# Hybrid decoder layer on one core: transposes of the SSD features pinned behind later matmul groups, early low parts on VectorE, first q and k projection traced ahead of the SSD output projection

## Chip, cores and metric

One core of a Trainium2 chip runs the whole kernel in one launch. The metric is the device time of that core in microseconds (us), lower is better.

## What is computed

One layer, 512 tokens, width 1024, float32 in and out. In short:

```python
proj = rms_norm(x) @ w_in                      # z | x,B,C | dt | q | k | v | f
y_ssd = ssd_mixer(xbc, z, dt)                  # conv(4) + silu, chunked scan, gate, group norm
y_fox = fox_mixer(q, k, v, f)                  # 16 heads, causal softmax with forget gates
x = x + concat(y_ssd, y_fox) @ w_out
x = x + conv_gated_mlp(rms_norm(x), w_up, w_down)
```

The SSD mixer has two groups of 8 heads. Its features (x, B, C: 1536 columns) go through a causal convolution over four tokens and a silu; then four chunks of 128 tokens are scanned one after the other, and the result is gated by silu(z) and normalised.

## The kernel before

**Matmuls in three passes.** Each float32 operand is split into a high part `h` (rounded to fp32r) and a low part `l` (the rest). `mm3` (line 108) issues h·h, h·l and l·h. `load_split` (line 99) brings one 128x1024 block of weights (512 KB) on SP's queue into `wraw` (5 buffers), ScalarE casts it to `wh` (line 104), and VectorE or GpSimd subtracts to give `wl` (line 105); `wh` and `wl` have 3 buffers each. Which engine subtracts is read, call by call, from the letters in the table `LOW_PART` (line 35): d is VectorE (DVE), p is GpSimd (POOL), and a key that is not in the table gives p. So the key feat (feature tiles) uses POOL for its first call only, z0 (the z projection of group 0, four blocks) has no entry and uses POOL four times, z1 is pdpd, o0 is d, and qk0 has no entry: four times POOL.

**The order of the work.** The program is traced in the order of the Python code, but it is not issued in that order: the framework's scheduler simulates the engines and picks, on each engine, the ready instruction of highest priority (earlier traced is higher; what is inside `urgent()` is raised by 2000). What it fixes is the order of each engine's queue. On the chip an engine takes its queue strictly in that order, and an instruction at the head that is not ready holds up the rest.

**The stages around the change.**

- Four feature tiles are made early (line 604, 605): j = 8 (B of group 0), 10 (C of group 0), 0 and 1 (x).
- `ssd_proj(g)` (line 338) goes over six feature tiles of group g: B, C, then four x tiles. Each is 24 matmuls of 512 columns, then on VectorE a multiply (L347), three taps of the convolution (L354) and the last step of the silu (L359), with two activations on ScalarE between (L350, L358). B and x are then transposed to token order: four PE transposes into one PSUM bank `xT` (lines 361 to 363; the pool `po` has a single bank), copied out by ScalarE (L368 for x, L370 for B). After the six tiles come two calls of `token_block` (line 321) for z, each 96 matmuls of 256 columns on two weight blocks, whose results are gated into `gz` (L377 to L379).
- `ssd_scan(g)` (line 388, urgent) runs the four chunks. Chunk c loads its row of decays (`sc`, L398), masks it on POOL (L407), takes exponentials (L412), multiplies (L415), then PE `yd` (L418), `yo` (L424), `st` (L431), VectorE steps on `y` and `xdt` (L421, L429, L439), and at the end the PE transposes `yT` (L449), which ScalarE and VectorE write into the operand pair `msh`, `msl` (L451, L452). That pair has one buffer: scan 1 writes it only when `out_proj((0, 1), m0)` has read the result of scan 0.
- `dt_f` (line 265) is a VectorE chain that ends in the decays `cs`, on which every chunk waits.
- The lines 604 to 623 fix the tracing order: early tiles, dt_f, ssd_proj(0), scan 0, ssd_proj(1), out_proj((0, 1), m0), scan 1, then `project(0)` (q and k of the first head group, two token_blocks, evacuated by L463, L465, L466, L471 and a power on POOL, L123) and `project_v(0)`. After that the attention heads follow (from L498 on), with the remaining projections as filler work, then the MLP.

Of the kernel before, what the change touches and what calls it, by code (L numbers as in the profile page):

```python
# [8 lines left out]
F32 = mybir.dt.float32  # L9
# [6 lines left out]
P = 128  # L16
# [3 lines left out]
NTB = SEQ // P  # L20
# [12 lines left out]
AHEAD = 2000  # L33
WARM = 8
LOW_PART = {
    "feat": "pddddddddp",
    "o0": "d",
    "o2": "d",
    "o4": "pd",
# [16 lines left out]
def tile_hybrid_layer(  # L56
# [20 lines left out]
    act, dve, pool, pe = nc.scalar, nc.vector, nc.gpsimd, nc.tensor  # L77
# [5 lines left out]
    po = ctx.enter_context(tc.tile_pool(name="po", bufs=1, space=PSUM))  # L83
# [42 lines left out]
    ident = cp.tile([P, P], F32, tag="ident", name="ident")  # L126
# [77 lines left out]
    for k in range(NK):  # L204
        pe.matmul(pdt[:64, :], wdt[:, k, :], xh[:, k, :], start=k == 0, stop=False, skip_group_check=True)
        pe.matmul(pdt[:32, :], wdt[:, k, 0:32], xl[:, k, :], start=False, stop=k == NK - 1, skip_group_check=True)
        c = slice(k * P, (k + 1) * P)
# [8 lines left out]
    def feature_tile(src, o=None):  # L216
        h, l = src if isinstance(src, tuple) else load_split(src, sub=low_part("feat"))
        o = bank() if o is None else o
        for k in range(NK):
            mm3(  # L220
                o, h[:, k * P : (k + 1) * P], l[:, k * P : (k + 1) * P], xh[:, k, :], xl[:, k, :],
                k == 0, k == NK - 1,
            )
        return o
# [13 lines left out]
    def out_proj(pairs, m, halves=(0, 1)):  # L238
        for half in halves:
            ws = [load_split(wout[pair, half], sub=low_part("o%d" % pairs[0])) for pair in pairs]  # L240
            banks = {}
            for t0 in (0, 2):
                for n, (h, l) in enumerate(ws):
                    for tb in (t0, t0 + 1):
                        s = slice(tb * P, (tb + 1) * P)
                        if n == 0:
                            banks[tb] = bank("po")
                        for j in range(2):
                            k = 2 * n + j
                            c = slice(j * 512, (j + 1) * 512)  # L250
                            mm3(
                                banks[tb], m[k][0][:, s], m[k][1][:, s], h[:, c], l[:, c],
                                k == 0, k == 2 * len(pairs) - 1,
                            )
                        if n == len(ws) - 1:
                            dst = x2[:, tb, half * 512 : (half + 1) * 512]
                            dve.tensor_add(dst, banks[tb], dst)
# [4 lines left out]
    def tmp(tag, name):  # L262
        return pss.tile([P, 512], F32, tag=tag, name=name, bufs=4 if tag == "t" else 2)
# [54 lines left out]
        act.activation(eacs, tokS[:, 1, :, 0:16], AF.Exp)  # L318
        nc.sync.dma_start(dsk, ssd_d[0:1, :].to_broadcast([P, SSD_HEADS]))

    def token_block(src, key="tb"):
        tiles = [bank("pq") for _ in range(2)]
        for kh in range(2):
            h, l = load_split(src[kh], sub=low_part(key))
            for b in range(2):
                for j in range(4):
                    k = 4 * kh + j
                    for c in range(2):
                        tb = 2 * b + c
                        s = slice(tb * P, (tb + 1) * P)  # L330
                        mm3(
                            tiles[b][:, c * 256 : (c + 1) * 256], xh[:, k, s], xl[:, k, s],
                            h[:, j * 256 : (j + 1) * 256], l[:, j * 256 : (j + 1) * 256],
                            k == 0 and c == 0, k == NK - 1, grouped=False,
                        )
        return tiles

    def ssd_proj(g):
        x_tok = [pss.tile([P, 512], F32, tag="x_tok", name="x_tok", bufs=7) for _ in range(NTB)]
        bT = pss.tile([P, SEQ], F32, tag="bT", name="bT", bufs=2)  # L340
        cT = pss.tile([P, SEQ], F32, tag="cT", name="cT", bufs=2)
        b_tok = pss.tile([P, NTB, P], F32, tag="b_tok", name="b_tok", bufs=2)
        gz = [pss.tile([P, 512], F32, tag="gz", name="gz", bufs=6) for _ in range(NTB)]
        for j in [8 + g, 10 + g] + list(range(4 * g, 4 * g + 4)):
            o = early.pop(j, None) or feature_tile(wxbc[j])
            xp = tmp("t", "xp")
            dve.tensor_mul(xp, o, R)  # L347
            dst = bT if j in (8, 9) else cT if j > 9 else tmp("t", "xs")
            cw = C_SCW + 4 * j
            act.activation(  # L350
                dst, xp, AF.Identity, scale=half_w[:, cw + 3 : cw + 4], bias=half_w[:, C_SCB + j : C_SCB + j + 1]
            )
            for s in range(1, 4):
                dve.scalar_tensor_tensor(  # L354
                    out=dst[:, s:], in0=xp[:, : SEQ - s], scalar=half_w[:, cw + 3 - s : cw + 4 - s], in1=dst[:, s:],
                    op0=ALU.mult, op1=ALU.add,
                )
            act.activation(xp, dst, AF.Tanh)  # L358
            dve.scalar_tensor_tensor(out=dst, in0=xp, scalar=1.0, in1=dst, op0=ALU.add, op1=ALU.mult)  # L359
            if j < 10:  # L360
                t = po.tile([P, 512], F32, tag="o", name="xT")
                for c in range(NTB):
                    pe.transpose(t[:, c * P : (c + 1) * P], dst[:, c * P : (c + 1) * P], ident)
                tv = t.rearrange("p (c f) -> p c f", c=NTB)
                if j < 8:
                    jj = j - 4 * g
                    for c in range(NTB):
                        act.copy(x_tok[c][:, jj * P : (jj + 1) * P], tv[:, c, :])  # L368
                else:
                    act.copy(b_tok, tv)  # L370
        for half in range(2):
            tiles = token_block(wz[2 * g + half], "z%d" % g)
            for tb in range(NTB):
                o = tiles[tb // 2][:, (tb % 2) * 256 : (tb % 2 + 1) * 256]
                dst = gz[tb][:, half * 256 : (half + 1) * 256]
                th = pss.tile([P, 256], F32, tag="th", name="th", bufs=2)
                act.activation(dst, o, AF.Copy, scale=rhalf[:, tb : tb + 1])  # L377
                act.activation(th, o, AF.Tanh, scale=rhalf[:, tb : tb + 1])
                dve.scalar_tensor_tensor(out=dst, in0=th, scalar=1.0, in1=dst, op0=ALU.add, op1=ALU.mult)  # L379
        return x_tok, bT, cT, b_tok, gz  # L380
# [220 lines left out]
    def urgent():  # L601
        return tc.high_priority(AHEAD)
# [5 lines left out]
    with urgent():  # L608
        m0 = ssd_scan(0, *st0)
    st1 = ssd_proj(1)  # L610
    out_proj((0, 1), m0)
    with urgent():
        m1 = ssd_scan(1, *st1)
    qk, vs = {}, {}

    def project(g):
        qk[g] = [qk_proj(g, 0), qk_proj(g, 1)]

    def project_v(g):
        vs[g] = v_proj(g)  # L620

    project(0)
    project_v(0)
    pss_ctx.close()
    pf_ctx = ExitStack()
# [51 lines left out]
    for half in range(2):  # L677
        c = slice(half * 512, (half + 1) * 512)
        ks = slice(half * 4, half * 4 + 4)
        for tb in range(NTB):  # L680
            s = slice(tb * P, (tb + 1) * P)
            with urgent():
                xw = pa.tile([P, 512], F32, tag="tok", name="xw", bufs=4)
                (dve if (half, tb) == (1, 3) else pool).tensor_tensor(out=xw, in0=x2[:, tb, c], in1=nw[:, c], op=ALU.mult)
                t = mbank("hT")
# [113 lines left out]
    for j in range(NH):  # L799
        g, val = gated(j)  # L800
# [180 lines left out]
```

## Time and profile before

| what | value |
|---|---|
| median of 3 runs | 815.75 us (815.62 to 817.22) |
| the profiled execution: its own time | 818.96 us |
| the profiled execution: span, first to last instruction | 817.2 us |
| granted TensorE clock | 0.999 |
| busy PE, DVE, ACT, POOL (us) | 803.1, 610.4, 437.2, 265.9 |

PE is the engine of the matmuls, PEld its weight loads, DVE is VectorE, ACT ScalarE, POOL GpSimd, SP the engine on whose queue the loads are issued. L12 is line 12 of the kernel. Names such as `xT<-ident,xs` give the tile that is written and those read. In a timeline each row has the start, the duration, the engine, line, operation, tiles, shapes and how many like instructions are merged; in brackets stands the idle time of the engine just before and what released it. Ends of matmuls are modelled: two matmuls that follow each other without a gap overlap in the rows, so the distance of two starts is the surer measure.

### The profile page before, as it was taken

To read this page: it belongs to the slowest core of one execution; us is meant where nothing else is said; L and a number is where in the kernel's file an instruction comes from. 1 tells how busy PE (TensorE), PEld (TensorE's weight loads), DVE (VectorE), ACT (ScalarE), POOL (GpSimd) and SP (SyncE) were. 2 spreads that over 40 slices of the span, in tenths; PEclk is the share of its full clock that TensorE was granted. 3 is DMA by queue.
4 is the path that set the end of the run, shared out by engine and by line. 5 is a ranking of instruction groups with operands and counts; after the bars stand their busy time and mean duration, and the time that the engine had idled before them with its cause. 6 is when DMAs were issued, how large, how long until landed. Compare 5 with 4: busy or idle time off the path is not lost.

```text
span 817.2 us, 12396 instructions
## 1 busy us (share of the span) xinstructions
PE 803.1 (98%) x4591; PEld 697.9 (85%) x4591; DVE 610.4 (75%) x987; ACT 437.2 (54%) x835; POOL 265.9 (33%) x268
## 2 busy tenths in 40 slices
PE   8989999999999999999999999999999999999997
PEld 6878878889999999898898888888888888888886
DVE  4696898656689898898996858666776666787844
ACT  7447656434387777585574364443444334556532
POOL 0233343255256635143211414333223333043120
PEclk9999999999999999999999999999999999999999
DMA  8524323323233433333321272233222322399983
GB/s 324 193 79 134 103 78 105 116 78 129 90 98 98 133 108 99 114 96 124 104 78 53 85 196 93 91 103 103 98 85 102 103 92 89 90 256 184 218 188 94
DMA packets 31404, 98.22 MB, mean 120 GB/s; under 512 B 4016, under 2 KB 5104, under 8 KB 31344
## 3 DMA queue, kind: packets, MB, share of 16 engines
q1 hardware_dynamic: 27456, 85.38, 32.1%
q0 software_dynamic: 3456, 11.54, 8.0%
q8 instruction: 36, 0.59, 0.3%
q10 hardware_dynamic: 432, 0.52, 0.2%
q14 instruction: 24, 0.20, 0.1%
HBM read 91.56 MB, written 2.20 MB: 115 GB/s over the span
## 4 chain that ended last, share of the span: by engine, by line
PE 85%; DVE 10%; DMA 2%; ACT 1%; issue 1%; POOL 0%; SPq 0%; DVEq 0%; ACTq 0%
PE up L111 29%; PE pq L111 19%; PE po L111 10%; PE Y L111 6%; PE X L111 4%; PE Z L111 4%; DVE xs L354 3%; PE o L587 2%; PE pT L573 2%; PE g L111 2%; PE S L547 1%; PE S L546 1%; DVE wl L105 1%; PE yd L418 1%; DVE xp L347 1%; DVE cT L354 1%
## 5 line engine op out<-in xcount | busy, mean ns | idle before, releaser
L104 ACT CAST wh<-wraw 128x1024 fp32r<-128x1024 f32 x103 | 108.5, 1053 | 141.2 <-PE up L111 78.6
L111 PE MATMUL pq<-wh,xl 128*128 128x256 f32 x512 | 148.3, 290 | 0.0
L111 PE MATMUL pq<-wh,xh 128*128 128x256 f32 x512 | 146.1, 286 | 0.0
L111 PE MATMUL pq<-wl,xh 128*128 128x256 f32 x512 | 145.7, 285 | 0.0
L111 PE MATMUL up<-hl,wh 128*128 128x512 f32 (+1 forms) x368 | 140.0, 381 | 0.0
L111 PE MATMUL up<-hh,wh 128*128 128x512 f32 (+1 forms) x368 | 139.9, 381 | 0.0
L111 PE MATMUL up<-hh,wl 128*128 128x512 f32 (+1 forms) x368 | 139.7, 380 | 0.0
L105 DVE TENSOR_TENSOR wl<-wraw,wh 128x1024 fp32r<-128x1024 f32 x81 | 104.0, 1284 | 32.3 <-ACT wh L104 27.9
L111 PEld LDWEIGHTS pq<-wh,xh 128*128 128x128 f32 x512 | 97.5, 190 | 2.1 <-issue 1.7
L111 PEld LDWEIGHTS pq<-wh,xl 128*128 128x128 f32 x512 | 97.5, 190 | 2.1 <-issue 1.4
L111 PEld LDWEIGHTS pq<-wl,xh 128*128 128x128 f32 x512 | 97.5, 190 | 0.6 <-issue 0.2
L111 PEld LDWEIGHTS up<-hl,wh 128*128 128x128 f32 x368 | 69.2, 188 | 13.4 <-issue 0.2
L111 PEld LDWEIGHTS up<-hh,wh 128*128 128x128 f32 x368 | 69.1, 188 | 13.3 <-issue 0.2
L111 PEld LDWEIGHTS up<-hh,wl 128*128 128x128 f32 x368 | 69.2, 188 | 13.1
L105 POOL TENSOR_TENSOR wl<-wraw,wh 128x1024 fp32r<-128x1024 f32 x22 | 54.0, 2459 | 71.8 <-ACT wh L104 57.2
L775 DVE TENSOR_TENSOR up<-up,R 128x512 f32<-128x512 f32 x44 | 30.3, 691 | 59.5 <-PE up L111 59.5
L780 DVE SCALAR_TENSOR_TENSOR ua<-up,pc,ua 128x511 f32<-128x511 f32 (+1 forms) x88 | 66.3, 758 | 1.4
L552 ACT ACTIVATE prob<-prob,nm 128x128 f32<-128x128 f32 (+1 forms) x64 | 35.9, 564 | 24.9 <-DVE nm L548 24.8
L736 ACT CAST wh<-T 128x1024 fp32r<-128x1024 f32 (+1 forms) x30 | 29.3, 977 | 36.8 <-PE Z L111 15.3
L737 DVE TENSOR_TENSOR wl<-T,wh 128x1024 fp32r<-128x1024 f32 (+1 forms) x30 | 33.7, 1133 | 19.1 <-ACT wh L736 18.8
L533 POOL TENSOR_SCALAR bias<-cum,tokS 128x256 f32<-128x256 f32 (+1 forms) x32 | 22.9, 725 | 71.6 <-DVE nm L548 71.6
L790 POOL TENSOR_TENSOR ua<-ua 128x512 f32<-128x512 f32 x11 | 15.0, 1363 | 92.6 <-DVE ua L780 92.6
(236 smaller groups left out, 1848.0 us busy)
## 6 DMA issues: line engine op xcount, KB each, us to landing
wraw<-in_wup_dram SPq DMA_DIRECT2D x44, 512.0 KB, 3.3
wraw<-in_wqkv_dram SPq DMA_DIRECT2D x24, 512.0 KB, 3.3
T<-in_wdown_dram POOLq DMA_DIRECT2D x20, 512.0 KB, 7.0
wraw<-in_wout_dram SPq DMA_DIRECT2D x16, 512.0 KB, 3.3
wraw<-in_wxbc_dram SPq DMA_DIRECT2D x11, 512.0 KB, 5.6
T<-in_wdown_dram SPq DMA_DIRECT2D x10, 512.0 KB, 5.5
wraw<-in_wdown_dram SPq DMA_DIRECT2D x10, 512.0 KB, 3.6
wraw<-in_wz_dram SPq DMA_DIRECT2D x8, 512.0 KB, 3.8
```

What stands on the lines that cost most here:

```text
L104: act.copy(h, r)
L105: (sub or dve).tensor_tensor(out=l, in0=r, in1=raw(h), op=ALU.subtract)
L111: ins = pe.matmul(o, a, b, start=start and n == 0, stop=stop and n == 2, **kw)
L354: dve.scalar_tensor_tensor(out=dst[:, s:], in0=xp[:, : SEQ - s], scalar=half_w[:, cw + 3 - s : cw + 4 - s], in1=dst[:, s:], op0=ALU.mult, ...
L533: (dve if qb == 2 else pool).tensor_scalar(out=b, in0=cum[:, :n], scalar1=-1.0, scalar2=edge, op0=ALU.mult, op1=ALU.add)
L552: act.activation(p, p, AF.Exp, scale=-1.0, bias=nm[:, qb : qb + 1], accum_out=sm[:, qb : qb + 1])
L573: pe.transpose(t[:, w : w + P], prob[:, o : o + P], ident)
L587: pe.matmul(cols[:m], v[:, kb, lh, vc], pt[:, s], start=kb == 0 and n == 0, stop=kb == NTB - 1, skip_group_check=True,)
L736: act.copy(h[:, :n], src[:, :n])
L737: dve.tensor_tensor(out=l[:, :n], in0=src[:, :n], in1=raw(h[:, :n]), op=ALU.subtract)
L775: dve.tensor_mul(xp, o, R2)
L780: dve.scalar_tensor_tensor(out=a[:, s:], in0=xp[:, : SEQ - s], scalar=pc[:, cw + 2 - s : cw + 3 - s], in1=a[:, s:], op0=ALU.mult, op1=ALU.add,
```

## The change

It has three parts. First, `LOW_PART` has only d for feat and for z0. Second, the transposes of B and x are no longer traced right after each tile: a queue `late` holds them, and each set of four is traced behind a later group of matmuls and pinned there. The pin (`keep_in_program_order`) is an edge of the order in PE's queue to the instruction that was traced just before; it fixes the earliest place in the queue, not the latest. B goes behind the group of the third x tile, the first x tile behind the group of the fourth, the other three x tiles behind pieces of the z projection (a piece is 24 matmuls, numbered 0 to 7 over both halves): pieces 1, 3 and 6 for group 0, pieces 1, 3 and 5 for group 1. Third, `project(0)` is traced ahead of `out_proj((0, 1), m0)` and of scan 1.

```diff
@@ LOW_PART
-    "feat": "pddddddddp",
+    "feat": "d",
+    "z0": "d",
@@ def token_block
-    def token_block(src, key="tb"):
+    def token_block(src, key="tb", behind=None):
...
                             k == 0 and c == 0, k == NK - 1, grouped=False,
                         )
+                if behind is not None:
+                    behind(2 * kh + b)
         return tiles
@@ def ssd_proj
-        for j in [8 + g, 10 + g] + list(range(4 * g, 4 * g + 4)):
+        def to_tokens(j, src):
+            t = po.tile([P, 512], F32, tag="o", name="xT")
+            for c in range(NTB):
+                tc.keep_in_program_order(
+                    pe.transpose(t[:, c * P : (c + 1) * P], src[:, c * P : (c + 1) * P], ident)
+                )
+            tv = t.rearrange("p (c f) -> p c f", c=NTB)
+            if j < 8:
+                jj = j - 4 * g
+                for c in range(NTB):
+                    act.copy(x_tok[c][:, jj * P : (jj + 1) * P], tv[:, c, :])
+            else:
+                act.copy(b_tok, tv)
+
+        late = []
+        for n, j in enumerate([8 + g, 10 + g] + list(range(4 * g, 4 * g + 4))):
             o = early.pop(j, None) or feature_tile(wxbc[j])
+            if n > 3:
+                to_tokens(*late.pop(0))
             xp = tmp("t", "xp")
...
             if j < 10:
-                t = po.tile([P, 512], F32, tag="o", name="xT")
-                for c in range(NTB):
-                    pe.transpose(t[:, c * P : (c + 1) * P], dst[:, c * P : (c + 1) * P], ident)
...
+                late.append((j, dst))
         for half in range(2):
-            tiles = token_block(wz[2 * g + half], "z%d" % g)
+            tiles = token_block(
+                wz[2 * g + half], "z%d" % g,
+                lambda piece: to_tokens(*late.pop(0)) if 4 * half + piece in (1, 3, 5 if g else 6) else None,
+            )
@@ the order of tracing
     st1 = ssd_proj(1)
+    qk, vs = {}, {}
...
+    project(0)
     out_proj((0, 1), m0)
     with urgent():
         m1 = ssd_scan(1, *st1)
-    qk, vs = {}, {}
...
-    project(0)
     project_v(0)
```

## Rows read from the trace of the kernel before

**Rows 1.** The page's busy time of each engine: busy us, share of the span, instructions.
```profile
PE 803.1 (98%) x4591; PEld 697.9 (85%) x4591; DVE 610.4 (75%) x987; ACT 437.2 (54%) x835; POOL 265.9 (33%) x268
```

**Rows 2.** Busy time of each engine in stretches of the span: start and end in us, length, then busy us (and instructions) of PE, PEld, DVE, ACT, POOL, the granted clock, the DMA share and GB/s.
```profile
40.00:60.00 20.00, 17.06 (x113) 15.29 (x112) 19.68 (x34) 8.69 (x16) 6.36 (x4) 1.00 0.25 80
...
80.00:140.00 60.00, 57.55 (x331) 48.32 (x331) 54.27 (x72) 35.47 (x88) 20.77 (x15) 1.00 0.29 99
140.00:230.00 90.00, 90.00 (x635) 82.19 (x635) 54.83 (x87) 39.53 (x90) 36.83 (x27) 1.00 0.29 97
230.00:340.00 110.00, 110.00 (x852) 105.73 (x851) 98.70 (x225) 83.53 (x192) 56.35 (x76) 1.00 0.38 111
340.00:465.00 125.00, 124.53 (x786) 110.09 (x785) 105.87 (x218) 71.86 (x153) 33.64 (x41) 1.00 0.30 93
```

**Rows 3.** PE's timeline between 47 and 70 us: the z projection of group 0 (`pq`) and the transposes `xT`.
```profile
47.83 0.27 PE L111 MATMUL pq<-wh,xh 128*128 128x256 f32 x1
...
49.97 0.28 PE L111 MATMUL pq<-wh,xh 128*128 128x256 f32 x1
50.09 0.28 PE L111 MATMUL pq<-wl,xh 128*128 128x256 f32 x1
51.88 0.66 PE L363 MATMUL xT<-ident,xs 128*128 128x128 f32 x4 [1.52 <-ACT b_tok L370]
...
57.56 0.66 PE L363 MATMUL xT<-ident,xs 128*128 128x128 f32 x4 [1.42 <-ACT x_tok L368]
...
64.07 0.63 PE L363 MATMUL xT<-ident,xs 128*128 128x128 f32 x4 [1.41 <-DVE xs L359]
...
69.26 0.60 PE L363 MATMUL xT<-ident,xs 128*128 128x128 f32 x4
```

**Rows 4.** PE's timeline further on: the waits of over half a microsecond between 80 and 235 us.
```profile
119.33 0.63 PE L363 MATMUL xT<-ident,xs 128*128 128x128 f32 x4 [1.26 <-ACT wh L104]
...
125.79 2.00 PE L418 MATMUL yd<-xdt,sc 128*128 128x64 f32 x16 [0.59 <-DVE sc L415]
...
132.65 1.10 PE L431 MATMUL st<-xdt,b_tok 128*128 128x512 f32 x2 [0.53 <-DVE xdt L429]
```

**Rows 5.** DVE's timeline: the long rows between 36 and 62 us, and before or behind them rows of the same kind of instruction; the first is a low part on DVE, the second the instruction that follows it.
```profile
31.21 1.23 DVE L105 TENSOR_TENSOR wl<-wraw,wh 128x1024 fp32r<-128x1024 f32 x1 [4.20 <-PE rbc L144]
32.35 1.28 DVE L347 TENSOR_TENSOR xp<-g,R 128x512 f32<-128x512 f32 x2
...
36.53 0.73 DVE L354 SCALAR_TENSOR_TENSOR xs<-xp,half_w,xs 128x511 f32<-128x511 f32 x1
...
37.60 2.96 DVE L354 SCALAR_TENSOR_TENSOR cT<-xp,half_w,cT 128x510 f32<-128x510 f32 x1
...
45.22 0.69 DVE L359 SCALAR_TENSOR_TENSOR cT<-xp,cT 128x512 f32<-128x512 f32 x1
...
46.43 2.29 DVE L359 SCALAR_TENSOR_TENSOR xs<-xp,xs 128x512 f32<-128x512 f32 x1
...
53.37 2.04 DVE L294 TENSOR_TENSOR e<-e,den 128x128 f32<-128x128 f32 x1
...
55.94 0.28 DVE L296 TENSOR_TENSOR q<-e 128x128 f32<-128x128 f32 x1
...
58.92 2.89 DVE L354 SCALAR_TENSOR_TENSOR xs<-xp,half_w,xs 128x509 f32<-128x509 f32 x1
```

**Rows 6.** POOL's timeline between 20 and 62 us: the low part of the second x tile, then the four of z0.
```profile
22.82 2.54 POOL L105 TENSOR_TENSOR wl<-wraw,wh 128x1024 fp32r<-128x1024 f32 x1 [0.44 <-ACT wh L104]
37.63 2.39 POOL L105 TENSOR_TENSOR wl<-wraw,wh 128x1024 fp32r<-128x1024 f32 x1 [12.27 <-DVE u L286]
45.70 2.47 POOL L105 TENSOR_TENSOR wl<-wraw,wh 128x1024 fp32r<-128x1024 f32 x1 [5.68 <-ACT wh L104]
52.86 2.41 POOL L105 TENSOR_TENSOR wl<-wraw,wh 128x1024 fp32r<-128x1024 f32 x1 [4.69 <-ACT wh L104]
58.54 2.73 POOL L105 TENSOR_TENSOR wl<-wraw,wh 128x1024 fp32r<-128x1024 f32 x1 [3.27 <-ACT wh L104]
```

**Rows 7.** DVE's timeline: the multiply of the decays of chunk 2 of scan 0, on which the `yd` of rows 4 waits.
```profile
124.52 1.21 DVE L415 TENSOR_TENSOR sc<-sc,cb 128x1024 f32<-128x1024 f32 x1
```

**Rows 8.** PE at the SSD output projection (`po`): its first matmul, the last chunk's transposes of scan 0, the first chunk's of scan 1, the first matmul of q and k, and the last chunk's transposes of scan 1.
```profile
153.97 0.40 PE L111 MATMUL po<-wh,msh 128*128 128x512 f32 x1
...
155.60 0.60 PE L449 MATMUL yT<-ident,y 128*128 128x128 f32 x4
...
178.97 0.60 PE L449 MATMUL yT<-ident,y 128*128 128x128 f32 x4
...
180.32 0.28 PE L111 MATMUL pq<-wh,xh 128*128 128x256 f32 x1
...
228.88 0.60 PE L449 MATMUL yT<-ident,y 128*128 128x128 f32 x4
```

**Rows 9.** ScalarE's timeline: the first write of scan 1's result.
```profile
180.34 0.59 ACT L451 CAST msh<-yT 128x512 fp32r<-128x512 f32 x1 [0.80 <-PE po L111]
```

**Rows 10.** POOL's timeline: the mask of a chunk of scan 1 at the head of the queue, the low part of q and k behind it, and the power for the norm of q.
```profile
169.00 1.09 POOL L407 TENSOR_SCALAR_AFFINE_SELECT sc<-sc 128x1024 f32<-128x1024 f32 x1 [11.66 <-DVE dte L405]
170.06 2.38 POOL L105 TENSOR_TENSOR wl<-wraw,wh 128x1024 fp32r<-128x1024 f32 x1
...
197.82 2.92 POOL L123 TENSOR_TENSOR ms<-ms,mhalf 128x16 f32<-128x16 f32 x1 [2.51 <-DVE ms L122]
```

More of the change, by code (lines that the diff above doesn't have):

```diff
@@ L360, in ssd_proj @@
             if j < 10:
-                t = po.tile([P, 512], F32, tag="o", name="xT")
-                for c in range(NTB):
-                    pe.transpose(t[:, c * P : (c + 1) * P], dst[:, c * P : (c + 1) * P], ident)
[L364 to L370, printed above, removed]
+                late.append((j, dst))
         for half in range(2):
-            tiles = token_block(wz[2 * g + half], "z%d" % g)
+            tiles = token_block(
+                wz[2 * g + half], "z%d" % g,
+                lambda piece: to_tokens(*late.pop(0)) if 4 * half + piece in (1, 3, 5 if g else 6) else None,
+            )
             for tb in range(NTB):
@@ L610, in tile_hybrid_layer @@
     st1 = ssd_proj(1)
-    out_proj((0, 1), m0)
-    with urgent():
-        m1 = ssd_scan(1, *st1)
     qk, vs = {}, {}
@@ L622, in tile_hybrid_layer @@
     project(0)
+    out_proj((0, 1), m0)
+    with urgent():
+        m1 = ssd_scan(1, *st1)
     project_v(0)
```

## The prediction

> **What bounds the kernel now.** I read the page's busy time first: PE has 803.1 of 817.2 us [rows 1], so what is not PE work is 14 us in all, and a change that leaves the matmuls as they are can win only from PE's waits. Then the stretches [rows 2]: between 140 and 340 us PE is busy all the time, and it loses 0.5 us between 340 and 465; the losses lie ahead of 140, where PE has 17.06 of 20 us (40 to 60) and 57.55 of 60 us (80 to 140) while DVE is the fullest engine beside it (19.68 of 20 and 54.27 of 60). So I went through PE's timeline there. Three of the four sets of x transposes of group 0 come after 1.52, 1.42 and 1.41 us of idle PE [rows 3], 4.35 us together; later one set of group 1, a `yd` and an `st` of scan 0 wait 1.26, 0.59 and 0.53 us [rows 4], 2.38 us. That is 6.73 us. The idle numbers are a little short, since ends of matmuls are modelled: the first wait is 50.09 to 51.88 from start to start, 1.79 us where 49.97 to 50.09 shows 0.12 as usual, so 1.67 and not 1.52. With 0.15 more for each of six waits, 7.6 us is all that there is to win.
>
> Next, why the transposes are late. The releasers are ScalarE's copies out of the single `xT` bank and DVE's last step of the silu, so DVE's chain is behind, and DVE's timeline shows where it lost time [rows 5]: a tap of the convolution takes 2.96 us where its neighbour takes 0.73, a silu step 2.29 instead of 0.69, a small multiply 2.04 (its like: 0.28), another tap 2.89. Each of the four begins within 0.8 us of one of POOL's low parts of z0, which run 37.63, 45.70, 52.86 and 58.54 us, for 2.39 to 2.73 us [rows 6]. So while POOL subtracts, DVE stands still: 2.23 + 1.60 + 1.76 + 2.15 = 7.7 us lost. PE's queue order was fixed by a simulation; that PE waits at these transposes says that DVE runs later on the chip than there.
>
> **Part 1, five low parts from POOL to DVE.** Removed: the 7.7 us of DVE standing still. Added: four low parts on DVE at 1.14 us (31.21 to 32.35, start to start [rows 5]), 4.6 us. DVE's chain of the x tiles and of `cs` ends 7.7 − 4.6 = 3.1 us earlier, though it takes work on. The fifth (the second x tile, 22.82 us on POOL [rows 6]) meets a DVE that stands idle 4.20 us before 31.21 [rows 5]: nothing. The `wl` of z0 is there 1.2 us sooner; PE did not wait for it. And the planner, which did not see the standing still, now sees 4.6 us more of DVE work, so it puts what hangs on DVE later into PE's queue, while on the chip DVE is 3.1 us earlier: the two come 7.7 us nearer. That is more than the 4.35 us of waits in this stretch, so I take these waits as gone: 4.35 + 3 × 0.15 = 4.8 us. Bounds: 0 and 4.8.
>
> What the page of the Trainium skill "SBUF — State Buffer", section Who interferes with whom, says of this: a DVE instruction with two SBUF inputs and a GpSimd instruction that reads SBUF exclude each other, and whichever comes second blocks until the first has finished. By it each low part would cost DVE POOL's whole instruction, 10.0 us for the four, and DVE would come out 5.4 us earlier instead of 3.1; the rows show less, and in the first pair it is DVE's row that starts first (37.60 against 37.63), yet DVE that is long. I go by the rows.
>
> **Part 2, the pins.** No instruction is added; the order of 40 transposes moves. Counting z0's matmuls from 47.83 at 0.12 us each, without the waits and the transposes, the four x sets of group 0 stand behind about 20, 50, 88 and 122 of them [rows 3]. The new earliest places are 0, 48, 96 and 168. So the pins move nothing for the first two sets (they rest on part 1), move the third by 8 × 0.12 = 1 us, and the fourth, which did not wait, by 46 × 0.12 = 5.5 us. That later `x_tok` is needed by chunk 0 of scan 0 only for `yd`, which also waits for the decays. In group 1 the waiting set of 119.33 [rows 4] is held until 48 matmuls of z1 are through, 5.8 us: that wait goes, 1.4 us. The other two of rows 4 hang on DVE in scan 0, not on the transposes; I leave them, 1.4 us with the 0.15 each. Price of holding x longer: the `xs` tiles keep three of the four buffers of their tag through the end of the group; the last tile's `xs` then waits for a set that stands just behind its own matmuls, 4 × 0.11 us. PE has z1 ahead of it then: nothing on the path.
>
> **Part 3, q and k ahead of the output projection.** The same instructions in another order: 4 loads of 512 KB on SP, 4 casts, 4 low parts of 2.4 us and two powers of 2.92 us on POOL [rows 10], 192 matmuls (192 × 0.12 = 23.0 us) and their evacuation move ahead of 4 loads, 4 casts, 4 low parts on DVE and 96 matmuls of `po`. SP's and POOL's queue is the risk. In POOL's queue a low part of q and k stood behind a mask that waited 11.66 us for DVE [rows 10]; three `wh`/`wl` buffers put a block two blocks of 48 × 0.12 = 5.8 us ahead of PE, so up to 11.5 us of that are hidden: 0 to 2 us, I take 0. DVE, which the four low parts stop, has 35 us free between 140 and 230 [rows 2]. What it gives: PE need no longer have scan 0's result when it has finished z1. Before, `po` began at 153.97 and the last `yT` of scan 0 came at 155.60 [rows 8], just in time; with PE some 6 us earlier and scan 0 only 3 us, `po` would have waited, for up to the difference. Without this part I would take back up to 3 us; with it, 0.
>
> **Sum.** 4.8 + 1.4 = 6.2 us less, and 0.5 us for new small waits of the sizes in rows 4, since every queue is ordered anew: 5.7. The profiled execution took 818.96 us (span 817.2 and 1.8 around it); it would take 813.3. It stands 3.2 us above the median of the runs shown, 815.75, from which the same sum gives 810.05: **810.0 us**. All waits gone is 815.75 − 7.6 = 808.1.
>
> **Rivals.**
>
> *A, the wait moves on to scan 0.* DVE is at 54.27 of 60 us between 80 and 140 [rows 2] and has no room there; `yd` of chunk 2 waited for the multiply that ended at 125.7 [rows 4, 7]. If scan 0 keeps its place among PE's matmuls, PE can be no earlier there than DVE, which gains 3.1 us: 812.6. Against it: the planner sees DVE later and has 23 us more of free matmuls to put ahead. Chance 0.20.
>
> *B, DVE becomes the bound.* If the long rows are not POOL's doing, 4.6 us of work go onto an engine at 19.68 of 20 us, the chain ends 4.6 us later, and the waits of rows 3 stay; what is won is the 1.4 of part 2 and 1 us at the third set, against up to 4.6: 813.4 to 818, say 815.8. Against it: four long rows at four low parts. Chance 0.13. The Trainium skill's page "Perfetto Trace Analysis", section Optimizing Scalar/DVE Operations, speaks for this side: with DVE saturated, handing work to other engines may make sense, GpSimd among them; it adds that the shared read port may undo that. By its first half the result would be B's.
>
> *C, slower: scan 1 backs up behind the later output projection.* Scan 1 may write `msh` only when `po` has been read: 180.34, right at the end of `po` [rows 8, 9]. The end of `po` moves by 23.0 − 6.2 = 16.8 us, to 197. If ScalarE's queue then holds scan 1 at its first write, the last `yT` comes 16.8 us later than 228.88, and so do the attention heads. The next 23 us of q and k matmuls cover the gap once, but the heads then have that much less filler beside them, with DVE at 204.6 of 235 us [rows 2]. Of the 16.8, half to all is lost: 810.05 + 8.4 to 16.8, 818.5 to 826.9, say 821. It ends slower once more than 7.3 us are not covered. Against it: only the writes need `msh`, and the chunks' other steps can go on. Chance 0.12.
>
> **How the numbers follow.** The forecast has 0.55. About 0.2% (1.6 us) is what a measurement of this kernel can tell from no change: below 814.1 is faster, above 817.4 slower. Faster: 0.53 of the forecast, 0.16 of A, 0.03 of B: 0.72. Same: 0.02, 0.04 and 0.07: 0.13. Slower: 0.03 of B and all of C: 0.15. The range reaches from all waits gone, with 0.5 us for the spread of the runs, to most of B: 807.6 to 816.5, leaving out C and a part of B; the forecast's own is 808.1 to 813.5.
>
> **What would show it.** Right: DVE's taps near 0.73 us throughout 36 to 62 us, POOL without L105 there, the three waits of rows 3 under 0.3 us, z0 ended near 73 instead of 78 us, `po` after q and k, PE still full to 340 us. Wrong: waits of PE at `yd` and `st` of scan 0 of 1 us or more each (A); transposes still waiting with DVE full (B); idle PE between 230 and 465 us, or a first `msh` write after 195 us with the next chunk behind it (C).

## The result, and the profile after

The changed kernel took **811.29 us** in the median of 4 runs (811.08 to 812.5), the kernel before 816.49 in the median of 4 on the same chip (815.62 to 818.53; three of these are the runs shown ahead of the prediction). The ratio is 0.9936, with a 95% interval of 0.9913 to 0.9959: faster by 5.2 us, where 5.7 were forecast. The profiled execution took 812.5 us with a span of 810.7, against 818.96 and 817.2.

The page's busy time, after; it answers to [rows 1]:

```profile
PE 800.7 (99%) x4591; PEld 697.2 (86%) x4591; DVE 608.0 (75%) x992; ACT 437.7 (54%) x835; POOL 257.0 (32%) x263
```

PE has the same 4591 matmuls. DVE has five instructions more (the five low parts, 5 × 1.22 = 6.1 us) and yet 2.4 us less of busy time in this execution. In the profiled execution of the same kernel in a later session it has 611.1 us, 0.7 more than before. So 5.4 to 8.5 us of standing still are gone, where 7.7 were counted. Span less PE's busy time is 14.1 us before and 10.0 after, so 4.1 of the 6.5 us between the two spans are waits of PE; the other 2.4 are PE's busy time, and the last section comes back to them.

The stretches after, with the busy time of PE, PEld, DVE, ACT and POOL in each (number of instructions in brackets), the granted clock, the DMA share and GB/s; they answer to [rows 2]:

```profile
40.00:60.00 20.00, 20.00 (x147) 18.89 (x146) 19.66 (x40) 12.79 (x28) 0.00 (x0) 1.00 0.30 102
80.00:140.00 60.00, 58.93 (x373) 51.58 (x372) 53.44 (x69) 34.22 (x85) 22.84 (x16) 1.00 0.28 97
140.00:230.00 90.00, 90.00 (x636) 82.21 (x635) 56.43 (x87) 40.79 (x93) 36.80 (x25) 1.00 0.32 102
230.00:340.00 110.00, 109.41 (x839) 104.46 (x838) 101.04 (x232) 82.25 (x189) 57.97 (x76) 1.00 0.37 110
340.00:465.00 125.00, 123.95 (x777) 109.14 (x776) 106.57 (x214) 73.30 (x156) 36.44 (x42) 1.00 0.31 91
```

PE is now full from 40 to 60 us; between 80 and 140 it loses 1.1 us where it lost 2.5; and it loses 0.6 and 1.1 us in the attention stage, where it lost nothing and 0.5. Which instructions wait is in PE's timeline after (start, duration, line, out<-in, idle before and its releaser); the first five lines are the sets of group 0, the next answer to [rows 4], the `po` to [rows 8]:

```profile
45.74 0.60 PE L352 MATMUL xT<-ident,bT 128*128 128x128 f32 x4
49.88 0.60 PE L352 MATMUL xT<-ident,xs 128*128 128x128 f32 x4
56.19 0.60 PE L352 MATMUL xT<-ident,xs 128*128 128x128 f32 x4
61.05 0.60 PE L352 MATMUL xT<-ident,xs 128*128 128x128 f32 x4
67.84 0.60 PE L352 MATMUL xT<-ident,xs 128*128 128x128 f32 x4
118.73 0.66 PE L352 MATMUL xT<-ident,xs 128*128 128x128 f32 x4 [0.47 <-ACT x_tok L358]
122.62 0.66 PE L464 MATMUL yT<-ident,y 128*128 128x128 f32 x4 [0.60 <-DVE y L459]
127.12 1.89 PE L433 MATMUL yd<-xdt,sc 128*128 128x64 f32 x16
132.65 1.02 PE L446 MATMUL st<-xdt,b_tok 128*128 128x512 f32 x2
172.56 0.40 PE L112 MATMUL po<-wh,msh 128*128 128x512 f32 x1
225.55 0.27 PE L464 MATMUL yT<-ident,y 128*128 128x128 f32 x1
256.30 0.30 PE L561 MATMUL S<-ks,qs 128*128 128x128 f32 x1 [0.51 <-DMA ks<-ks]
386.62 0.30 PE L561 MATMUL S<-ks,qs 128*128 128x128 f32 x1 [0.74 <-DMA ks<-ks]
```

No set of group 0 waits any more. The `yd` and `st` of scan 0, which were to keep their waits, have none; an `xT` and a `yT` ahead of them wait 0.47 and 0.60 us instead. Two score matmuls wait for the copy of `ks` by DMA. The idle times of 0.2 us and more that PE's timeline prints from 25 us on add up to 7.05 us before and 2.63 after.

DVE's timeline after, where [rows 5] had the four long rows:

```profile
36.20 0.75 DVE L375 SCALAR_TENSOR_TENSOR cT<-xp,half_w,cT 128x510 f32<-128x510 f32 x1
37.53 1.22 DVE L106 TENSOR_TENSOR wl<-wraw,wh 128x1024 fp32r<-128x1024 f32 x1
45.51 0.69 DVE L380 SCALAR_TENSOR_TENSOR xs<-xp,xs 128x512 f32<-128x512 f32 x1
52.03 0.28 DVE L295 TENSOR_TENSOR e<-e,den 128x128 f32<-128x128 f32 x1
60.21 0.74 DVE L375 SCALAR_TENSOR_TENSOR xs<-xp,half_w,xs 128x509 f32<-128x509 f32 x1
64.75 0.42 DVE L308 TENSOR_TENSOR_SCAN cs<-ones,ad 128x128 f32<-128x128 f32 x1
116.03 2.88 DVE L380 SCALAR_TENSOR_TENSOR xs<-xp,xs 128x512 f32<-128x512 f32 x1
```

The tap, the silu step and the small multiply have their usual 0.75, 0.69 and 0.28 us again. At 116.03 a silu step still takes 2.88, beside a low part of z1 in POOL's timeline:

```profile
115.53 2.83 POOL L106 TENSOR_TENSOR wl<-wraw,wh 128x1024 fp32r<-128x1024 f32 x1
```

It lies ahead of both waits that are left at 118 and 122 us.

### The profile page after: what moved, and what is told of

Its sections match the earlier page's. It is cut to its first block, busy times and chain, and to the rows that moved or that the text cites. A ratio compares the mean times of both kernels' runs of the same rounds, so it can differ in the third digit from the quotient of the medians.

```text
span 810.7 us, 12402 instructions
## 1 busy us (share of the span) xinstructions
PE 800.7 (99%) x4591; PEld 697.2 (86%) x4591; DVE 608.0 (75%) x992; ACT 437.7 (54%) x835; POOL 257.0 (32%) x263
## 4 chain that ended last, share of the span: by engine, by line
PE 87%; DVE 4%; DMA 3%; POOL 2%; issue 2%; ACT 1%; SPq 0%; DVEq 0%; POOLq 0%
PE up L112 30%; PE pq L112 19%; PE po L112 10%; PE Y L112 6%; PE X L112 4%; PE Z L112 4%; PE g L112 3%; PE o L602 2%; PE pT L588 2%; PE j L112 1%; PE yd L433 1%; DMA sc<-cs_d 1%; PE S L562 1%; PE S L561 1%; DVE xs L375 1%
## 5 line engine op out<-in xcount | busy, mean ns | idle before, releaser
L106 DVE TENSOR_TENSOR wl<-wraw,wh 128x1024 fp32r<-128x1024 f32 x86 | 110.2, 1281 | 25.3 <-ACT wh L105 21.3
L106 POOL TENSOR_TENSOR wl<-wraw,wh 128x1024 fp32r<-128x1024 f32 x17 | 42.1, 2474 | 59.8 <-ACT wh L105 56.2
L752 DVE TENSOR_TENSOR wl<-T,wh 128x1024 fp32r<-128x1024 f32 (+1 forms) x30 | 33.8, 1134 | 19.2 <-ACT wh L751 18.8
L548 POOL TENSOR_SCALAR bias<-cum,tokS 128x256 f32<-128x256 f32 (+1 forms) x32 | 25.9, 818 | 67.9 <-DVE nm L563 59.5
```

The source lines that it names most:

```text
L106: (sub or dve).tensor_tensor(out=l, in0=r, in1=raw(h), op=ALU.subtract)
L548: (dve if qb == 2 else pool).tensor_scalar(out=b, in0=cum[:, :n], scalar1=-1.0, scalar2=edge, op0=ALU.mult, op1=ALU.add)
L752: dve.tensor_tensor(out=l[:, :n], in0=src[:, :n], in1=raw(h[:, :n]), op=ALU.subtract)
```

## The experiments

Theory: POOL's low parts stop DVE, that makes the transposes late, and the other two parts only let PE keep what this wins. Rivals: the order in PE's queue (parts 2 and 3) wins by itself; or rivals A, B and C of the prediction. Six kernels are the six ways of making one or two of the three parts.

**Part 1 alone.**

```diff
-    "feat": "pddddddddp",
+    "feat": "d",
+    "z0": "d",
```

> Part 1 alone: the low parts of feat and z0 on VectorE, transposes and the order of projections as before. Theory (POOL's low part stops DVE, and that is what made the first transposes late): DVE's rows of 2 to 3 us between 36 and 62 us are gone, the three waits of PE in z0 (4.35 us idle) fall under 0.5 us together, and the time falls by 4 to 5 us, to a ratio of 0.994 to 0.995; the waits between 80 and 140 us stay at 2 to 3 us. Rival (it is the pins that clear them): waits in z0 of 3 us or more remain, ratio 0.998 or above. Rival B (DVE becomes the bound): DVE's chain ends later, ratio 1.000 or above.

816.15 us against 818.23, ratio 0.9974 (0.9958 to 0.999), where 0.994 to 0.995 was expected. The three waits of [rows 3] are gone by this part alone. Less is won than expected: PE waits at a new place. PE's timeline of this kernel:

```profile
119.46 0.66 PE L364 MATMUL xT<-ident,xs 128*128 128x128 f32 x4 [1.89 <-ACT x_tok L369]
155.03 0.63 PE L450 MATMUL yT<-ident,y 128*128 128x128 f32 x4 [1.64 <-DVE y L445]
156.58 0.50 PE L112 MATMUL po<-wh,msh 128*128 128x512 f32 x1 [0.70 <-ACT msh L452]
```

PE comes to the output projection before scan 0 is through and gives back 2.3 us there: what part 3 was costed at, up to 3 us, in a kernel without it. The clock may have a share too: of the twelve executions the three with a mean granted clock of 0.999 or 1.0 took 813.3 to 813.7 us, the nine with 0.994 to 0.997 took 814.6 to 819.8. The profile shown is one of the three; where the clock was lower in the others is not on record.

In this kernel the planner puts the four x sets of group 0 behind 29, 68, 132 and 160 matmuls of z0 (before: 20, 50, 87 and 121). So part 1 has two effects, DVE is earlier and PE comes to the sets later, and this run does not part them.

**Part 2 alone** (the transposes behind later matmul groups, the table of low parts and the order of the projections as before).

```diff
...
         for half in range(2):
-            tiles = token_block(wz[2 * g + half], "z%d" % g)
+            tiles = token_block(
+                wz[2 * g + half], "z%d" % g,
+                lambda piece: to_tokens(*late.pop(0)) if 4 * half + piece in (1, 3, 5 if g else 6) else None,
+            )
```

> Part 2 alone: transposes pinned behind later groups, low parts of z0 on POOL, order of projections as before. Theory (part 1 clears the waits in z0, the pins only those of group 1): the long DVE rows stay; the first two of the three waits in z0 stay at 1.4 us each, the third shrinks by 1 us; the wait of 1.26 us at 119 goes: 2 to 2.5 us in all, ratio 0.997. Rival (the pins clear them): z0 without waits, ratio 0.994 or less.

823.85 us against 818.23, ratio 1.0062 (1.0042 to 1.0083): slower, where a gain was expected. PE's timeline:

```profile
50.65 0.66 PE L351 MATMUL xT<-ident,xs 128*128 128x128 f32 x4 [1.51 <-ACT b_tok L359]
56.32 0.66 PE L351 MATMUL xT<-ident,xs 128*128 128x128 f32 x4 [1.42 <-ACT x_tok L357]
62.82 0.63 PE L351 MATMUL xT<-ident,xs 128*128 128x128 f32 x4 [0.33 <-DVE xs L379]
64.78 0.38 PE L309 MATMUL pt<-cs,carry 128*128 128x1 f32 x2 [0.73 <-DVE cs L307]
113.68 1.10 PE L445 MATMUL st<-xdt,b_tok 128*128 128x512 f32 x2 [1.62 <-DVE xdt L443]
125.47 1.12 PE L463 MATMUL yT<-ident,y 128*128 128x128 f32 x4 [3.59 <-DVE y L458]
```

In group 0 it is as counted: the first two sets don't move and wait as before, the third waits 1.1 us less. But the time that it gives back is waited for at the next instruction that hangs on DVE, and in group 1 the wait of the `xT` is gone while an `st` and a `yT` wait 1.62 and 3.59 us. The `y` that the latter waits for is a long row of DVE again, beside a low part of POOL. DVE's timeline and then POOL's:

```profile
122.59 2.82 DVE L458 SCALAR_TENSOR_TENSOR y<-y,ss,nwb 128x512 f32<-128x512 f32 x1 [0.46 <-POOL ss L123]
```
```profile
122.52 2.34 POOL L105 TENSOR_TENSOR wl<-wraw,wh 128x1024 fp32r<-128x1024 f32 x1
```

The printed idle times of PE make 11.06 us, 4.0 more than before; measured are 5.6. The rest is in the granted clock. The stretches of this kernel around that wait, columns as above:

```profile
122.00:124.00 2.00, 0.00 (x0) 0.00 (x0) 1.54 (x2) 0.00 (x0) 2.00 (x2) 1.00 0.68 258
124.00:126.00 2.00, 0.53 (x3) 0.53 (x4) 2.00 (x2) 0.00 (x0) 0.86 (x1) 0.60 0.13 25
128.00:130.00 2.00, 2.00 (x11) 2.00 (x10) 2.00 (x4) 1.44 (x4) 0.00 (x0) 0.50 0.00 0
```

After the wait the granted clock is 0.50, the 1.2 GHz level, until about 131 us. The z1 matmuls start 0.21 us apart from 126.67 to 131.3 instead of 0.12: some 22 of them, 0.09 us each, 2.0 us; the four `yT` and two `cb` just ahead are 0.1 each slower, 0.6 us. With that the sum is 6.6, where this trace is 6.7 longer from the first matmul into `j` on. Over all six executions it shows as well: the one with a mean granted clock of 0.998 took 820.16 us, the five with 0.990 to 0.993 took 822.91 to 824.9.

**Part 3 alone.**

```diff
...
+    project(0)
     out_proj((0, 1), m0)
     with urgent():
         m1 = ssd_scan(1, *st1)
...
-    project(0)
     project_v(0)
```

> Part 3 alone: q and k of the first head group traced ahead of the SSD output projection. Theory: no wait of the kernel before hangs on it, so 0 to 0.5 us either way, ratio 0.9995 to 1.0005, with po after q and k and PE full between 140 and 340 us. Rival C (scan 1 backs up behind the later output projection): the last yT of scan 1 comes 10 us or more later than 229 us and the heads lose 3 us or more, ratio 1.004 or above.

818.8 us against 818.23, ratio 1.001 (0.9997 to 1.0022): no difference that can be told. All waits of before are there (1.52, 1.43 and 1.40 us at the sets of group 0). Rival C needs scan 1 to stop behind its first write of `msh`. ScalarE's timeline of this kernel:

```profile
212.91 1.56 ACT L451 CAST msh<-yT 128x512 fp32r<-128x512 f32 x3 [0.73 <-PE po L111]
```

The writes do wait for `po`, three of them together, but the last `yT` stands at 229.0 us (before: 228.88 [rows 8]): only the writes are held, not the scan.

**Parts 1 and 2**, and **parts 1 and 3** (the edits as above, two at a time).

> Parts 1 and 2 without part 3: the SSD output projection comes straight after z1 again. Theory: the waits of z0 and that at 119 us are gone as with all three parts, but PE is then 5 to 6 us earlier at the output projection while scan 0 is only some 3 us earlier, so up to 3 us of waits show between 140 and 165 us (at po or at the scan's matmuls): ratio 0.994 to 0.997. Rival (part 3 does nothing): the time of all three parts, 0.9936 within 0.001, and no wait of PE between 140 and 165 us.

> Parts 1 and 3 without the pins. Theory (part 1 clears z0, the pins only the later wait of group 1): z0 without waits, a wait of a transpose of group 1 of 1 to 1.5 us between 110 and 135 us is there again or stands at the next yd; ratio 0.994 to 0.996. Rival (the pins do the main part): waits of 3 us or more in z0, ratio 0.998 or above.

813.49 us against 818.23, ratio 0.9944 (0.9924 to 0.9963), and 813.86 against 818.43, ratio 0.9946 (0.9927 to 0.9965). Without part 3 PE waits 1.53 us at the `yT` of 156.30 and 0.56 at the `po` of 157.72, 2.1 us; with part 3 it waits for nothing between 140 and 230. Without part 2 the `xT` of group 1 at 122.89 waits 2.01 us; with it an `xT` and a `yT` share 1.15. In both traces a fall of the granted clock follows such a wait, 0.50 from 158.5 to 161.9 us and from 123.7 to 127.2, and costs some 1.5 us more; these two executions took 816.81 and 816.77 us, some 3 us above the medians.

**Parts 2 and 3.**

> Parts 2 and 3, the low parts of feat and z0 on POOL as before. Theory (POOL's low part stops DVE): four DVE rows of 2 to 3 us between 36 and 62 us are back, and waits of PE of 3 to 4 us in z0 with them; ratio 0.997 to 0.998. Rival (the pins do the main part): z0 without waits although the long DVE rows are there, ratio 0.994 or less.

824.07 us against 818.43, ratio 1.0075 (1.0048 to 1.0101): slower again, a miss in the same way as part 2 alone. The long rows are back in DVE's timeline:

```profile
35.65 2.96 DVE L374 SCALAR_TENSOR_TENSOR cT<-xp,half_w,cT 128x510 f32<-128x510 f32 x1
44.48 2.29 DVE L379 SCALAR_TENSOR_TENSOR xs<-xp,xs 128x512 f32<-128x512 f32 x1
51.41 2.04 DVE L294 TENSOR_TENSOR e<-e,den 128x128 f32<-128x128 f32 x1
56.96 2.88 DVE L374 SCALAR_TENSOR_TENSOR xs<-xp,half_w,xs 128x509 f32<-128x509 f32 x1
```

The same four durations as in [rows 5] to 0.01 us, from another queue order, and the `yT` at 125.26 waits 3.59 us as in part 2 alone. So parts 2 and 3 gain nothing without part 1, and part 2 then costs 5.6 us.

**Low parts further to DVE**: all three parts, with the low parts of z1 and of the first q and k on DVE too (twice, the second time beside a repeat of the changed kernel), and with every low part on DVE.

```diff
-    "z1": "pdpd",
+    "z1": "d",
+    "qk0": "d",
```
```diff
-        return dve if order[n % len(order)] == "d" else pool
+        return dve
```

> All three parts, and the low parts of z1 (two on POOL) and of the first q and k (four on POOL) on VectorE too. Theory (a low part on POOL costs DVE about 1.9 us and on DVE 1.14): DVE's long rows between 100 and 140 us shrink, the waits of PE of 0.6 and 0.76 us there go, 0.5 to 1.5 us less than with the three parts: ratio to the kernel before 0.992 to 0.993. Rival (DVE is the bound between 80 and 140 us and the two more parts of 1.14 us weigh): waits of PE there of 2 us or more, ratio 0.995 or above.

> All three parts, and every low part of the kernel on VectorE, those of the attention stage too. Theory (POOL's low parts stop DVE): DVE's busy sum over the span, 608 us with the three parts, falls or stays, although it takes on 17 instructions of 1.2 us, and the time is that of the three parts or 0.5 to 1.5 us less. Rival (in the attention stage POOL's low parts run beside DVE steps that they don't stop, and DVE has 13 per cent left): DVE's busy sum rises by 10 us or more, and PE gets waits of 2 us or more between 230 and 465 us: ratio 0.996 or above.

> The three parts once more, beside the next kernel and on the same chip. Theory: 0.993 to 0.9945 of the kernel before, with the two waits near 118 and 122 us again, since the queue orders are the same.

> The three parts with the low parts of z1 and of the first q and k on VectorE too, beside the three parts on the same chip. Theory (the waits near 118 and 122 us hung on POOL's low parts of z1): 0.5 to 1.5 us less than the three parts alone. Rival (the difference seen is the head of the kernel, which varies by up to 3 us from run to run): within 0.4 us of them.

The first took 812.16 us against 818.43, ratio 0.9926 (0.9912 to 0.994), then 811.68 against 818.33, 0.9912 (0.9892 to 0.9933); the changed kernel beside that one 811.85, 0.992 (0.9902 to 0.9937). The two waits of 118 and 122 us go, as they should if POOL's low part of z1 makes them (0.29 at a `yd` in their place), but 0.2 us of medians does not tell the two kernels apart, where 0.5 or more was expected. The traces do: from the first matmul into `j` to the end of the span the changed kernel takes 787.4 and 787.5 us in its two profiled executions, this one 786.5 and 786.6. That is 0.9 us less, as expected; the medians also hold the start of the program, which differs by more than that from one execution to the next (last section). The kernel with every low part on DVE took 812.51 us against 818.43, 0.9928 (0.9911 to 0.9945). Its page:

```profile
PE 801.6 (99%) x4591; PEld 697.1 (86%) x4591; DVE 616.1 (76%) x1009; ACT 436.2 (54%) x835; POOL 218.1 (27%) x246
```

17 instructions more on DVE, at some 1.2 us each 20 us, raise its busy time by 8.1 over 608.0, and by 5.0 over the 611.1 of the later session; a fall or no change was expected. So POOL's 17 low parts had cost it 12 to 15 us, 0.7 to 0.9 each, not the 1.6 to 2.2 of [rows 5]. What one costs depends on what DVE runs beside it. PE's waits of 118 to 123 us are gone, and between 410 and 450 us three at `S` and `po` come instead (0.29, 0.49 and 0.60). From the first matmul into `j` on this kernel takes 787.4 us, as the changed one does, so the 0.9 us of z1, q and k are not left; the idle times (1.99 us here, 1.91 and 1.80 there) don't show where they go.

**The low parts of z0 cut**: in the kernel before, POOL takes 256 of the 1024 columns and DVE 768.

```diff
...
+        if cut:
+            pool.tensor_tensor(out=l[:, :cut], in0=r[:, :cut], in1=raw(h[:, :cut]), op=ALU.subtract)
+            dve.tensor_tensor(out=l[:, cut:], in0=r[:, cut:], in1=raw(h[:, cut:]), op=ALU.subtract)
+            return h, l
...
-            h, l = load_split(src[kh], sub=low_part(key))
+            h, l = load_split(src[kh], sub=low_part(key), cut=256 if key == "z0" else 0)
```

> The kernel before, with each low part of z0 cut: POOL subtracts 256 of the 1024 columns, DVE the other 768. Theory (DVE stands still for as long as POOL's subtraction runs): POOL's instruction takes about 0.65 us, and no DVE row between 36 and 62 us is more than 0.8 us longer than its like, against 1.6 to 2.2 us before; the three waits in z0 are gone or under 0.5 us together. Rival (DVE pays a fixed price whenever POOL starts a subtraction): DVE rows stay 1.5 us or more too long.

815.48 us in one run (818.33 before): the waits of the sets of group 0 are gone here too. POOL's timeline, then DVE's:

```profile
34.61 0.74 POOL L106 TENSOR_TENSOR wl<-wraw,wh 128x256 fp32r<-128x256 f32 x1 [9.42 <-DVE u L290]
40.16 1.19 POOL L106 TENSOR_TENSOR wl<-wraw,wh 128x256 fp32r<-128x256 f32 x1 [4.80 <-DVE bT L363]
46.48 0.88 POOL L106 TENSOR_TENSOR wl<-wraw,wh 128x256 fp32r<-128x256 f32 x1 [5.14 <-ACT wh L104]
52.35 0.74 POOL L106 TENSOR_TENSOR wl<-wraw,wh 128x256 fp32r<-128x256 f32 x1 [5.00 <-ACT wh L104]
```
```profile
34.59 1.31 DVE L358 SCALAR_TENSOR_TENSOR cT<-xp,half_w,cT 128x510 f32<-128x510 f32 x1
40.78 0.71 DVE L291 TENSOR_TENSOR u<-u,R 32x128 f32<-32x128 f32 x1
46.68 1.23 DVE L358 SCALAR_TENSOR_TENSOR xs<-xp,half_w,xs 128x510 f32<-128x510 f32 x1
52.41 0.68 DVE L351 TENSOR_TENSOR xp<-g,R 128x512 f32<-128x512 f32 x1
```

Three DVE rows are too long by 0.56, 0.43 and 0.49 us (their likes 0.75, 0.28 and 0.74), beside POOL rows of 0.74 to 1.19. Four whole low parts cost 7.7 us, four quarters 1.5: it is no fixed price. It goes by what is left of POOL's instruction when the DVE row starts. In [rows 5] and [rows 6] the long DVE rows start 2.42, 1.74, 1.90 and 2.35 us ahead of the end of POOL's row, and lose 2.23, 1.60, 1.76 and 2.15; here it is 0.76, 0.57 and 0.68, and they lose 0.56, 0.43 and 0.49. In all seven the loss is 0.14 to 0.20 less than what was left. The fourth has no long row beside it: what DVE runs there reads `g` from PSUM.

This run also answers, for the first set, what part 1 alone left open: it stands behind 22 matmuls of z0 here, hardly later than the 20 of before, and its wait of 1.68 us (from start to start) is gone. The second and third stand behind 62 and 125, later by 12 and 38; how much of their waits the later place takes, and how much the earlier DVE, is not parted by any run.

## Why the prediction was right, point by point

**Part 1: mechanism and size right, one step of its working wrong.** 4.8 us were forecast for the three waits of [rows 3]; from start to start they were 1.68, 1.58 and 1.57, 4.83, and all went; z0's last matmul starts 5.0 us earlier, counted from the first matmul into `j` (48.4 us after it instead of 53.4). That POOL's low parts cause them is shown both ways: they go with part 1 alone and with quarter-width low parts, and are there in the kernels without part 1 (with the pins, the third set's in part at a later instruction). The working had both DVE being earlier and the planner putting the sets later, and both are there: counted from the first `xp`, the four x tiles are ready 1.1, 1.0, 5.6 and 3.6 us earlier, and their sets stand 9, 28, 28 and 47 matmuls further back. The prediction took the page "SBUF — State Buffer" of the Trainium skill, section Who interferes with whom, to price each low part at POOL's whole instruction, 10.0 us. The Trainium skill says less there, only that whichever of the two comes second blocks until the first has finished. By that the four rows of [rows 5] would stand for the 8.4 us that were left of POOL's rows, and they lost 7.7; with quarters 2.0 and 1.5. So the trace agrees but for 0.14 to 0.20 us a row, and but for the two pairs where DVE's row starts 0.02 to 0.03 us ahead by the profile (37.60 and 34.59) and is held all the same. The Trainium skill's statement there that a DVE instruction with at most one SBUF input, outside the 2-port perf modes, doesn't contend agrees with the row at 52.41 of the last kernel, 0.68 us beside POOL.

The step that failed is "DVE's chain of the x tiles and of `cs` ends 3.1 us earlier". Counted from the first `xp` of group 0 (32.35 before, 30.95 after), the fourth x tile was ready after 32.6 us instead of 36.2, 3.6 earlier; but the scan that makes `cs` began after 33.8 instead of 32.7, 1.1 later, and `cs` with its carry, which also waits for a matmul, after 37.9 instead of 35.0. In the new order of DVE's queue four gating steps of z (0.42 us each; from 56.83 us on), the next low part (1.23 us, at 61.51) and the last steps of the fourth x tile stand ahead of it, which all came after it before. No wait of PE shows it: the matmul that reads `cs`, at 68.52 us, does not wait, and no `yd` waits 0.2 us or more.

**Part 2: too much by about half, the places wrong, and worth something only with part 1.** 1.4 us were forecast from the `xT` of [rows 4], and 1.4 were to stay at `yd` and `st`. From start to start the waits between 80 and 140 us went from 3.1 to 1.4, 1.7 less; but `yd` and `st` lost theirs and the `xT` kept a part. Not all of that is part 2: with parts 1 and 3 and without it, PE waits 2.01 us there, with it 1.07, and without part 3 it is 1.89 and 1.15. So beside part 1 it takes off 0.7 to 0.9 us of waits; the medians of the kernels with and without it do not settle it, since the intervals of parts 1 and 3 and of all three overlap. The count of the places (20, 50, 96 and 168 matmuls ahead of the sets of group 0) is what part 2 alone shows; with all parts they stand at 29, 78, 115 and 168, and with part 1 alone at 29, 68, 132 and 160: the planner, which now sees the low parts as DVE's work, moves the sets further than the pins ask. That was said of the planner, but not put into the count.

**Part 3: right.** "Up to 3 us taken back without it, 0 with it": 2.3 and 2.1 us in the two kernels that lack it and have part 1, none in those that have both, and nothing measurable by itself. What was not forecast is that such a wait can be followed by a lower clock, some 1.5 us more in the trace of parts 1 and 2.

**New small waits: undersized.** 0.5 us were set; the attention stage lost 1.2 us more than before by PE's busy time, some 1.5 from start to start, most of it at two `S` that wait for `ks` by DMA (0.51 and 0.74), one of which waited 0.15 before. What sets the time of those copies wasn't tried.

**The sum.** 4.8 + 1.7 − 1.5 = 5.0 us of waits from start to start, where 4.8 + 1.4 − 0.5 = 5.7 were forecast; from the first matmul into `j` to the end of the span the two traces differ by 5.1. The small waits were undersized by 1.0 and the stage from 80 to 140 us by 0.3. That the latter comes so near is in part luck: with part 1 alone the waits of that stage are 2.1 already, so 1.0 of the 1.7 is part 1's, where none was forecast for it.

**The rivals.** A, a wait that moves on to scan 0, did not happen to the whole change, but it is what happens to the pins without part 1: 1.62 and 3.59 us at `st` and `yT`. It was put at less gain; with the clock after it, it is a loss of 5.6 us. B fell: DVE took 6.1 us of work on, its busy time changed by −2.4 and +0.7 us in the two profiled executions, and its x tiles of group 0 were ready earlier. The Trainium skill's "Perfetto Trace Analysis", section Optimizing Scalar/DVE Operations, has both halves of it, and the second, that the shared port may undo an offload to GpSimd, is the one that the runs bear out. C fell: `po` did move to 172.56 us and the first `msh` write to 201.72, after the 195 us that were named as its sign, but the last `yT` of scan 1 came at 225.55, earlier than before.

The table sets the traces beside the medians, as differences to the kernel before. The second column is the sum of PE's printed idle times, the third what matmuls at the lower granted clock cost in the middle of the program, the fourth the time from the first matmul into `j` to the end of the span:

| parts | idle of PE, us | clock, us | from `j` to the end, us | medians, us |
|---|---|---|---|---|
| 1 | −1.4 | 0 | −2.5 | −2.1 |
| 2 | +4.0 | +2.6 | +6.7 | +5.6 |
| 3 | +2.3 | 0 | +3.2 | +0.6 |
| 1, 2 | −2.1 | +1.5 | −1.3 | −4.7 |
| 1, 3 | −3.1 | +1.5 | −2.8 | −4.6 |
| 2, 3 | +3.7 | +1.5 | +6.4 | +5.6 |
| 1, 2, 3 | −4.4, −4.2 | 0 | −5.1, −5.0 | −5.2, −6.5 |

Idle times and clock give the fourth column to 1.2 us; the idle times are short by some 0.15 us a wait. Two executions of the same kernel agree in it to 0.1 us (all three parts, 787.40 and 787.49). The medians are of other executions: the profiled ones of part 3, of parts 1 and 2 and of parts 1 and 3 took some 3 us more than their medians, and a median also has the start of the program in it.

## What to carry to other kernels

Where a DVE row is several times as long as its likes, look for a POOL row that is running while it starts (within 0.8 us of its own start in [rows 6]); moving that work onto the "full" engine can empty it. A queue order that was worked out without this stop is wrong by its sum, 7.7 us here, and shifting instructions in it moves the wait on to the next one that hangs on the same engine. What frees one engine must be followed to its next meeting with the other: here 2 us of the gain would have been lost at `po`, had nothing been put ahead of it.

## What the runs showed of the hardware that was not expected

A wait of PE can cost more than itself, since the granted clock may fall behind it. After the 3.59 us wait it was 0.50, the 1.2 GHz level, from 124.4 to 131.2 us with part 2 (some 2.6 us lost) and from 126.7 to 130.1 with parts 2 and 3 (1.5). But it also fell after shorter ones: after 2.01 us at the `xT` with parts 1 and 3, after 1.53 and 0.56 us at `yT` and `po` with parts 1 and 2, and after 1.66 and 0.70 at the same place with quarter-width low parts. With part 1 alone PE waits 1.64 and 0.70 us there and the clock stays, as it does after the 1.5 us waits of [rows 3]. So the length of the wait alone does not tell. The stretch behind `po`, with parts 1 and 2 and with part 1 alone:

```profile
158.00:160.00 2.00, 2.00 (x7) 1.57 (x7) 1.01 (x2) 0.00 (x0) 0.06 (x1) 0.62 0.20 54
```
```profile
158.00:160.00 2.00, 2.00 (x11) 1.59 (x10) 0.00 (x0) 0.00 (x0) 0.00 (x0) 1.00 0.00 0
```

The start of the program differs from run to run by more than this change is worth in one part: the first matmul into `j` came at 24.72 us before, 23.32 after, 21.97 in part 1 alone and 25.30 in parts 1 and 3, though this stretch has hardly an edit. Matmuls of 512 columns start 0.43 us apart there at first, for a longer or shorter time. The stretch from 10 to 12 us before, after, and in part 1 alone, one fence each:

```profile
10.00:12.00 2.00, 2.00 (x6) 1.25 (x6) 2.00 (x4) 2.00 (x4) 0.00 (x0) 1.00 1.06 405
```
```profile
10.00:12.00 2.00, 2.00 (x7) 1.33 (x6) 2.00 (x4) 2.00 (x4) 0.00 (x0) 0.60 1.04 403
```
```profile
10.00:12.00 2.00, 2.00 (x11) 1.40 (x9) 2.00 (x5) 2.00 (x4) 0.00 (x0) 1.00 1.07 412
```

Six, seven and eleven matmuls in 2 us, at 1.00, 0.60 and 1.00 granted. The first 1.00 is no reading: the clock's records in that trace begin only at 13.89 us. Where there are records, the pace goes with them. With the changed kernel the granted clock is 0.50 from 8.2 to 11.6 us, and the step goes from 0.43 to 0.23 us at 11.66; with parts 1 and 3 it is 0.50 from 7.7 to 14.5, and the step changes at 14.56; with part 1 alone the records begin at 5.5 us with the full clock, and 512-column matmuls start 0.23 us apart from 8.1 on. In the kernel before the step changes at 13.95. The first matmul into `j` follows in the same order: 21.97, 23.32, 24.72 and 25.30 us. So the start differs by how long PE runs at the lower level there. That is 1.9 of the 2.4 us by which PE's busy time differs between the two profiled executions, and 1.4 us of the 6.5 between their spans come from there.
